# Reordering the branch units, output projection and first MLP pair of a one-core decoder layer

## The chip, the cores and the metric

The kernel runs on one core of a Trainium2 chip. The metric is the device time of one execution in microseconds (us), lower is better. Five engines work side by side, each through its own instruction stream: PE (TensorE, matrix products), DVE (VectorE), ACT (ScalarE), POOL (GpSimd) and SP (SyncE, which here only starts transfers). An engine runs its stream in order; an instruction that waits for another engine holds up everything behind it on its own.

## The reference

One decoder layer on x of 1024 positions by 1024 channels, float32. Two token mixers, gated and merged, are projected by w_out and added to x; a gated MLP with a causal convolution of width 3 follows.

```python
merged = (jax.nn.sigmoid(g_a) * (y_att @ w_oa[l])
          + jax.nn.sigmoid(g_b) * (y_sgu @ w_ob[l]))
x = x + merged @ w_out[l]
x = x + conv_gated_mlp(rmsnorm(x, ffn_norm[l]), w_up[l], conv_w[l], conv_b[l], w_down[l])
```

## The kernel before

Every large product is done in a form with 7 block products instead of 8 (Strassen's scheme in Winograd's form). The left operand, a weight, comes as the blocks A11, A12, A22 and the sums S1 to S4, the right operand as B11, B21, B22 and the sums T1 to T4. The results of the block products are added up on DVE and ACT into the four quarters of the output. Each factor is stored as a high part in a short format and the low rest of it, and a product is three matmuls (high by high, high by low, low by high), each 128x128 by 128x512. To **split** a tile means: ACT copies it into the short format (the high part, `copy_hi`, line 88), then DVE or POOL subtracts that from the tile (the low part). All weights' low parts are made on POOL.

The change touches three stages, which follow each other on PE.

**Branch units, u0 to u7** (`branch`, order in `B_UNITS`). Each computes two tiles of 128 output channels of one branch ("a" or "b") and multiplies them by the gate. A unit is two jobs, `first` (products A11, S3, A12, S1) and `second` (A22, S2, S4). The names follow the products: `x1` and `x7` are ACT's copies of the first two out of PSUM, `u2` that of a partial sum. A12 adds onto the bank that x1 copies, so PE can't begin A12 before the x1 copy (L1360) is done. In branch "a" (u2, u4, u6, u7) the unit's result must be added to branch "b"'s, tile by tile: `m_add` puts the sum into `mraw`, the merged activations. It does so late, in the first job of the next unit or, for u7, in output job 0 (`un["late"]`). `mraw` is the right operand of the output projection, so its blocks B11, B21, B22 and the sums T1 to T4 are formed from it (`m_sum`) and split (`m_split`), in halves 0 and 1 of two tiles each. Where such work stands in the streams is written by hand: `un["hooks"][u, 0]` and `[u, "x"]` run at two places of unit u's first job, `[u, 1]` at the end of its second, and `O_WORK[j]` in output job j.

**Output jobs 0 to 13** (`out_job`). Step s (0 to 6, `O_STEPS`) is one of the seven block products, job 2s + e does its tiles 2e and 2e + 1, with 24 matmuls. The results gather in two PSUM accumulators, pX and pY. `o_post` takes one to its end: `final` adds it (times plus or minus one half) to the tiles of x in `ac`, `keep` copies the new x back into `ac` and stores it to memory, and the gained tiles become the right operand of the MLP (`comb`): `right_hi`/`right_lo` for B21 and B22, `right_split` for B11, T1, T3, T2 and T4, held until then in the buffers A and B (tiles hA and hB) and in pX and pY. `square` squares the new x on ACT and adds it up on POOL, for the normalization. Job j also splits the weights of job j + 2 (`wjh` on ACT, `wjl` on POOL). In between stands the preparation of the first MLP pair's weights (`w0`): loads that add two blocks in memory, issued by POOL (`adds`), their sums `lr` (`sums_r`) and the splits ph/pl, s3h/s3l and qh/ql.

**The first MLP pair** (`first_pair`, then a pair of the steady kind that takes over from it). Products in order: A11·B11, S3·T3, S1·T1, A12·B21, S4·B22, S2·T2, A22·T4. ACT copies the first out (`x1f`), the second (`x7`) and the third (`u2`; both are `xu`), DVE subtracts x7 - u2 and adds x1f to the fourth (L1775), and S4·B22 adds onto that. `fax` is the low part of the weights for S2 and S4.

Jobs run in a fixed pattern (`run_jobs`): PE's matmuls of job i, the load of job i + 4, the split of job i + 2, and then what DVE and ACT do with the result.

## Time and profile before

| | |
|---|---|
| median of 3 runs | 1204.44 us (1203.92 to 1204.49) |
| profiled execution | 1206.05 us, its span 1204.0 us |
| mean granted clock of PE | 0.989 |
| PE, DVE, POOL, ACT busy | 97%, 72%, 55%, 49% of the span |

In span time the branch units take about 379 to 457 us, the output jobs 457 to 545, the first pair and the one behind it 545 to 611. From there on all MLP pairs run alike, up to the down projection at the end. In the rows that follow later, a line such as `pz<-y,wjh` says that the tile pz was written from y and wjh; x2 behind a shape is a group of two such instructions; a bracket says how long the engine had been idle and which engine and line ended that. "PE pz L1106 <- ACT x L1360: 5.1, 2, 2.6" is a wait: PE's product at line 1106 waited for ACT's copy at line 1360, 5.1 us in two times, the longest 2.6.

### The profile page before, as it was taken

Reading aid. Unit: us, or ns where it says so; the run is one execution under the profiler, and the core shown is the slowest. Engines: PE = TensorE matmul, PEld = TensorE weight load, DVE = VectorE, ACT = ScalarE, POOL = GpSimd, SP = SyncE. Lnnn points to the kernel's source line nnn. Section 1 sums busy time; section 2 is a strip of 40 time slices with the busy share of each in tenths; the row PEclk is TensorE's granted clock in tenths of the full one; section 3 lists DMA queues with packets and bytes.
Section 4 is the critical chain, followed back from the end, with each engine's and each line's share of the span. In section 5 each row is a group of like instructions: output and inputs, shape, how many; then the busy total and the mean of one; then the engine's idle time right before and its main releaser. Section 6 shows DMA issues by size and latency. Waiting matters only on the chain.

```text
span 1204.0 us, 15874 instructions
## 1 busy us (share of the span) xinstructions
PE 1169.4 (97%) x5784; PEld 985.9 (82%) x5784; DVE 860.9 (72%) x1007; ACT 592.5 (49%) x938; POOL 657.0 (55%) x460
## 2 busy tenths in 40 slices
PE   9999999999999999896999999999999999999998
PEld 9899999888888777684878888888888887888886
DVE  7777737635447779676487878878887798776674
ACT  6665668644346444656444444444444445435331
POOL 1677774688865545574877776767767541000000
PEclk9999999999999999998999999999999999999999
DMA  9332584175647645533454455545545257975561
GB/s 369 127 115 73 136 250 172 62 245 163 169 137 263 197 173 210 182 107 122 92 172 126 137 165 136 167 115 151 154 136 149 85 201 271 370 250 192 159 234 53
DMA packets 86430, 204.37 MB, mean 170 GB/s; under 512 B 9617, under 2 KB 17297, under 8 KB 86161
## 3 DMA queue, kind: packets, MB, share of 16 engines
q1 hardware_dynamic: 77280, 174.93, 42.0%
q0 software_dynamic: 8544, 19.93, 10.0%
q10 hardware_dynamic: 528, 8.52, 2.1%
q8 instruction: 45, 0.74, 0.2%
q14 instruction: 33, 0.26, 0.1%
HBM read 162.70 MB, written 57.41 MB: 183 GB/s over the span
## 4 chain that ended last, share of the span: by engine, by line
PE 71%; DVE 14%; ACT 5%; POOL 4%; issue 3%; DMA 2%; SPq 0%; DVEq 0%; ACTq 0%; POOLq 0%
PE pz L1106 42%; PE pd L1984 7%; PE pdx L1984 7%; PE pu L94 1%; PE pu L92 1%; PE pu L93 1%; PE pY L1632 1%; DVE tv L1682 1%; DVE tg L1682 1%; PE pq L92 1%; PE pq L94 1%; PE pq L93 1%; PE pv L560 1%; DVE pz L664 1%; DVE mraw L1440 1%
## 5 line engine op out<-in xcount | busy, mean ns | idle before, releaser
L1106 PE MATMUL pz<-T,qh 128*128 128x512 f32 x472 | 145.5, 390 | 0.0
L1106 PE MATMUL pz<-B,ph 128*128 128x512 f32 x352 | 110.9, 397 | 1.5 <-ACT x L1818 0.8
L1106 PEld LDWEIGHTS pz<-T,qh 128*128 128x128 f32 x472 | 88.4, 188 | 18.6 <-ACT u L930 0.3
L1065 POOL TENSOR_TENSOR pl<-lp,ph 128x1024 fp32r<-128x1024 f32 x30 | 73.3, 2443 | 49.7 <-ACT ph L88 49.7
L1106 PE MATMUL pz<-T,ql 128*128 128x512 f32 x236 | 91.8, 389 | 0.0
L1106 PEld LDWEIGHTS pz<-B,ph 128*128 128x128 f32 x352 | 65.6, 189 | 18.1 <-ACT x L1818 3.9
L1106 PE MATMUL pz<-T,s3h 128*128 128x512 f32 x232 | 72.9, 396 | 6.1 <-ACT x1f L1754 6.1
L1106 PE MATMUL pz<-y,wjh 128*128 128x512 f32 x224 | 72.0, 403 | 5.5 <-ACT x L1360 5.1
L1124 DVE TENSOR_TENSOR pz<-pz,rstd_b 128x1024 f32<-128x1024 f32 x60 | 73.9, 1232 | 4.6 <-ACT rstd_b L143 2.6
L1065 POOL TENSOR_TENSOR ql<-lq,qh 128x1024 fp32r<-128x1024 f32 x30 | 76.7, 2556 | 0.0
L1106 PE MATMUL pz<-B,pl 128*128 128x512 f32 x176 | 69.3, 394 | 2.3 <-POOL pl L1065 2.3
L1984 PE MATMUL pdx<-bh,al 128*128 128x512 f32 x176 | 68.7, 390 | 0.2 <-DVE al L1955 0.2
L1984 PE MATMUL pdx<-bh,ah 128*128 128x512 f32 x176 | 68.6, 390 | 0.1
L1984 PE MATMUL pdx<-bl,ah 128*128 128x512 f32 x176 | 68.5, 389 | 0.0
L1346 POOL TENSOR_TENSOR wjl<-wj,wjh 128x512 fp32r<-128x512 f32 (+1 forms) x32 | 40.3, 1279 | 45.1 <-ACT wjh L88 45.1
L1106 PE MATMUL pz<-T,AX 128*128 128x512 f32 x252 | 60.5, 389 | 0.0
L1106 PE MATMUL pz<-B,AX 128*128 128x512 f32 x252 | 60.5, 389 | 0.0
L1065 POOL TENSOR_TENSOR s3l<-lq,s3h 128x512 fp32r<-128x512 f32 x20 | 25.9, 1297 | 62.5 <-ACT s3h L88 62.5
L88 ACT ACTIVATE ah<-ra 128x1024 fp32r<-128x1024 f32 (+1 forms) x24 | 23.7, 988 | 68.8 <-DMA ra<-wdown 30.6
L1106 PEld LDWEIGHTS pz<-T,s3h 128*128 128x128 f32 x232 | 44.4, 192 | 16.1 <-ACT x1f L1754 6.8
L88 ACT ACTIVATE AX<-lr 128x1024 fp32r<-128x1024 f32 x21 | 22.3, 1063 | 71.1 <-POOL lr L664 71.1
L1682 DVE SCALAR_TENSOR_TENSOR tv<-pz,cp,tv 128x1023 f32<-128x1023 f32 (+1 forms) x44 | 56.2, 1278 | 0.8
(380 smaller groups left out, 3629.7 us busy)
## 6 DMA issues: line engine op xcount, KB each, us to landing
lp<-wup SPq DMA_DIRECT2D x22, 512.0 KB, 3.8
lq<-wup SPq DMA_DIRECT2D x22, 512.0 KB, 4.1
ra<-wdown SPq DMA_DIRECT2D x44, 256.0 KB, 4.4
b<-T SPq DMA_DIRECT2D x44, 256.0 KB, 3.4
lq<-wup POOLq DMA_DIRECT2D x42, 256.0 KB, 5.4
B<-tv SPq DMA_DIRECT2D x33, 256.0 KB, 2.0
T<-tt SPq DMA_DIRECT2D x33, 256.0 KB, 2.1
b<-B SPq DMA_DIRECT2D x33, 256.0 KB, 3.0
```

The source lines that it names most:

```text
L88: return nc.scalar.activation(dst, src, AF.Copy, scale=scale)
L92: nc.tensor.matmul(out, wh, mh, start=first, stop=False, **kw)
L93: nc.tensor.matmul(out, wh, ml, start=False, stop=False, **kw)
L94: nc.tensor.matmul(out, wl, mh, start=False, stop=last, **kw)
L560: nc.tensor.matmul(o, vhl[:, kb, g, :], w[:, 2 * g:2 * g + 2, :], start=i == 0 and g == 0, stop=i == len(ops) - 1, skip_group_check=True)
L664: eng.tensor_tensor(out, x, y, op=op)
L1065: nc.gpsimd.tensor_tensor(l, r, h.bitcast(F), op=ALU.subtract)
L1106: nc.tensor.matmul(o, p[:, k, :], m, start=not more and k == 0 and j == 0, stop=k == nk - 1 and j == 2, skip_group_check=True)
L1124: nc.vector.tensor_tensor(z, z, rstd_b, op=ALU.mult)
L1346: nc.gpsimd.tensor_tensor(l[:, k], r[:, k], h[:, k].bitcast(F), op=ALU.subtract)
L1682: nc.vector.scalar_tensor_tensor(t[:, j:], p[:, 0:1024 - j], cw[:, ci, 2 - j:3 - j], t[:, j:], op0=ALU.mult, op1=ALU.add)
L1984: nc.tensor.matmul(o[d], p[:, k - k0, m], q[:, k - k0, :], start=new and k == 0 and j == 0, stop=k == HK - 1 and j == 2, skip_group_check= ...
```

## The change

It moves operations to other places of the streams of ACT, DVE and POOL; the matmuls and their order stay.

- Branch units: the split of B11 and the T1 sum leave `m_add` for the end of the second job of the unit (`hooks[3, 1]`, `[5, 1]`), behind that unit's own sums; T1 is split at the end of u6 (`hooks[6, 1]`) instead of within u6's first job. B21 and the T2 sums go from `m_add` and u7's hook to output job 0.
- Output jobs: the sums for T3 and T4 go from job 2 to jobs 6 and 7, their splits to jobs 7 to 9; T2 is split in job 1; `w0.adds` goes from job 6 to 7, `split_s3` from 8 to 9, `sums_r` from 7 to 8.
- `final`, `keep`, `right_split`, `square` and the copies of pX to pY work on a pair of tiles (1024 columns) where they worked on one (512). The buffer `sqt` of the squares exists once, for a pair, where there were two for a tile each. The high part of an output weight is one copy instead of two.
- First pair: the four operations `B - g·22`, needed for T2, leave `o_post` for the place behind x1f and fax; `X + …`, needed for T4, goes behind the third product; T2's split goes behind x7's copy; a square stands behind fax, one behind u2's copy and one behind the fourth product.

```diff
@@ run_jobs
             if i == 16:
                 un["late"]()
+                m_lo("B21", 0)
+                for k in (slice(2, 3), slice(3, 4)):
+                    m_hi("B21", 1, k)
+                    m_lo("B21", 1, k)
+                m_sum("T2", 0)
+                m_sum("T2", 1)
@@ gates
-        un["hooks"][6, "x"] = lambda: m_split("T1", 0)
-        un["hooks"][6, 0] = lambda: m_split("T1", 1)
-        un["hooks"][7, 0] = lambda: (m_split("B22", 0), m_split("B21", 0))
+        un["hooks"][3, 1] = lambda: (m_split("B11", 0), m_sum("T1", 0))
+        un["hooks"][5, 1] = lambda: (m_split("B11", 1), m_sum("T1", 1))
+        un["hooks"][6, 1] = lambda: (m_split("T1", 0), m_split("T1", 1))
@@ m_add
-        if i == 0:
-            m_split("B11", g)
-        else:
-            if u == 7:
-                for e in (0, 1):
-                    m_split("B21", g, ks=slice(2 * g + e, 2 * g + e + 1))
-        m_sum(("T1", "T2")[i], g)
@@ square
-        if n in ("11", "12") and d == 0:
-            nc.scalar.activation(q, ob[n][:, d, :], AF.Square)
+        t = pools["fp"].tile([128, 2, 512], F, tag="sqt", name=nm("sqt"))
+        nc.scalar.activation(t, ob[n][:, 2 * e:2 * e + 2, :], AF.Square)
+        if n in ("11", "12") and e == 0:
+            nc.gpsimd.tensor_tensor(q, t[:, 0, :], t[:, 1, :], op=ALU.add)
         else:
-            t = pools["fp"].tile([128, 512], F, tag="sqt", name=nm("sqt"), bufs=2)
-            nc.scalar.activation(t, ob[n][:, d, :], AF.Square)
-            nc.gpsimd.tensor_tensor(q, q, t, op=ALU.add)
+            for k in (0, 1):
+                nc.gpsimd.tensor_tensor(q, q, t[:, k, :], op=ALU.add)
@@ O_WORK
-        0: lambda: (m_split("T2", 0), out_load("11"), out_load("21")),
-        1: lambda: (m_split("T2", 1), m_split("B22", 1), out_load("22")),
-        2: lambda: (m_sum("T3", 0), m_sum("T3", 1), m_sum("T4", 0), m_sum("T4", 1), out_load("12")),
-        3: lambda: m_split("T4", 0),
-        4: lambda: (square("11", 0), square("11", 1), w0.load_p(), w0.load_s3(), w0.load_q()),
-        5: lambda: (b11(0), b11(1), square("11", 2), square("11", 3)),
-        6: lambda: (b11(2), b11(3), w0.adds(), m_split("T4", 1)),
-        7: lambda: (m_split("T3", 0), w0.sums_r()),
-        8: lambda: (m_split("T3", 1), w0.split_s3()),
-        10: lambda: (square("12", 0), square("12", 1)),
-        11: lambda: (square("12", 2), square("12", 3)),
-        12: lambda: (square("22", 0), square("22", 1)),
-        13: lambda: (square("22", 2), square("22", 3)),
+        0: lambda: (m_hi("B21", 0), m_hi("B22", 0), out_load("11"), out_load("21")),
+        1: lambda: (m_split("T2", 0), m_split("T2", 1), m_lo("B22", 0), out_load("22")),
+        2: lambda: (m_split("B22", 1), out_load("12")),
+        4: lambda: (square("11", 0), w0.load_p(), w0.load_s3(), w0.load_q()),
+        5: lambda: (b11(0), square("11", 1)),
+        6: lambda: (b11(1), m_sum("T3", 0), m_sum("T3", 1)),
+        7: lambda: (m_split("T3", 0), w0.adds(), m_sum("T4", 0), m_sum("T4", 1)),
+        8: lambda: (m_split("T3", 1), m_split("T4", 0), w0.sums_r()),
+        9: lambda: (square("12", 0), m_split("T4", 1), w0.split_s3()),
+        10: lambda: square("12", 1),
+        12: lambda: square("22", 0),
@@ o_post, one tile at a time before, a pair after; steps 5 and 6
-            if s == 5:
-                right_lo("B22", d, Yb[d], gs[d][0])
-                stt(B[:, d, :], Yb[d], gs[d][1], B[:, d, :], ALU.subtract)
-                stt(Yb[d], Yb[d], gs[d][1], A[:, d, :], ALU.add)
-            if s == 6:
-                right_lo("B21", d, X[d], gs[d][0])
-                stt(X[d], X[d], gs[d][0], B[:, d, :], ALU.add)
+        if s in (5, 6):
+            m, p = ("B22", Yb) if s == 5 else ("B21", X)
+            for i, d in enumerate(ds):
+                right_hi(m, d, p[:, i, :], gs[i][0])
+            keep(n, e, p)
+            for i, d in enumerate(ds):
+                right_lo(m, d, p[:, i, :], gs[i][0])
+        if s == 5:
+            for i, d in enumerate(ds):
+                stt(Yb[:, i, :], Yb[:, i, :], gs[i][1], A[:, d, :], ALU.add)
@@ first_pair
         q.prod(q.v1, "A11", "B11")
-        for f in o_late:
-            f()
         nc.scalar.copy(x1, q.v1)
...
+        square("22", 1)
+        for d in range(4):
+            stt(ob["B"][:, d, :], ob["22"][:, d, :], gain("22", d)[1], ob["B"][:, d, :], ALU.subtract)
         nx.load_p()
         q.prod(q.v0, "S3", "T3")
-        for d in range(4):
-            right_split("T2", d, ob["B"][:, d, :], nc.vector)
         nc.scalar.copy(x7, q.v0)
+        for e in (0, 1):
+            right_split("T2", e, ob["B"][:, 2 * e:2 * e + 2, :])
...
         nc.scalar.copy(u2, q.g1)
+        square("21", 0)
+        for e in (0, 1):
+            for i in (0, 1):
+                d = 2 * e + i
+                p = ob["X"][e][:, i, :]
+                stt(p, p, gain("21", d)[0], ob["B"][:, d, :], ALU.add)
+            right_split("T4", e, ob["X"][e])
         sub(nc.vector, x7, x7, u2)
-        for d in range(4):
-            right_split("T4", d, ob["X"][d], nc.vector)
         q.prod(q.g0, "A12", "B21")
-        for d in range(4):
-            square("21", d)
+        square("21", 1)
```

The first place is DVE's stream around the second job of u3, whose merged rows come from u2. `mraw<-m,pz` are m_add's sums, `mB<-mraw,mB` is the low part of B11, `mraw<-mraw` the T1 sum, and from `pz<-x,pz` on these are the unit's own sums. Before:

```order
L1440 TENSOR_TENSOR mraw_4366<-m_4141,pz_4237 128x1024
L1440 TENSOR_TENSOR mraw_4366<-m_4143,pz_4238 128x1024
L1418 TENSOR_TENSOR mB_4369<-mraw_4366,mB_4369 128x1024
L664 TENSOR_TENSOR mraw_4366<-mraw_4366 128x2x512
L1380 TENSOR_TENSOR pz_4324<-x_562_4325,pz_4324 128x512
L664 TENSOR_TENSOR pz_4324<-pz_4324,u_564_4327 128x512
```

The same place of the changed kernel (its lines are numbered 6 to 13 higher):

```order
L1452 TENSOR_TENSOR mraw_4366<-m_4141,pz_4237 128x1024
L1452 TENSOR_TENSOR mraw_4366<-m_4143,pz_4238 128x1024
L1386 TENSOR_TENSOR pz_4324<-x_562_4325,pz_4324 128x512
L664 TENSOR_TENSOR pz_4324<-pz_4324,u_564_4327 128x512
L664 TENSOR_TENSOR pz_4324<-x_563_4326,pz_4324 128x512
L1392 TENSOR_TENSOR pz_4323<-u_564_4327,pz_4323 128x512
L1399 SCALAR_TENSOR_TENSOR m_4406<-th_4284,pz_4323 128x1024
L1399 SCALAR_TENSOR_TENSOR m_4408<-th_4286,pz_4324 128x1024
L1422 TENSOR_TENSOR mB_4410<-mraw_4366,mB_4410 128x1024
L664 TENSOR_TENSOR mraw_4366<-mraw_4366 128x2x512
```

The low part of B11 and the T1 sum moved behind all six of the unit's operations; on ACT the high part moved with them, from ahead of u2's copy to right ahead of the next x1 copy.

The second place is DVE's stream in output jobs 6 to 9. `ac<-pY,ac` is job 6's and 7's final, `mT` the low parts of T3 and T4. Before:

```order
L1418 TENSOR_TENSOR mT_5007<-mraw_4707,mT_5007 128x1024
L1513 SCALAR_TENSOR_TENSOR ac_4848<-pY_4895,ac_4848 128x512 x2
L1418 TENSOR_TENSOR mT_667_5185<-mraw_4366,mT_667_5185 128x1024
L1513 SCALAR_TENSOR_TENSOR ac_4848<-pY_4896,ac_4848 128x512 x2
L1418 TENSOR_TENSOR mT_667_5185<-mraw_4366,mT_667_5185 128x1024
L1513 SCALAR_TENSOR_TENSOR pY_4895<-pY_4895,ac_4848 128x512 x2
```

Changed:

```order
L664 TENSOR_TENSOR mraw_4366<-mraw_4706,mraw_4366 128x2x512 x2
L1525 SCALAR_TENSOR_TENSOR ac_4839<-pY_4888,ac_4839 128x1024
L1422 TENSOR_TENSOR mT_666_5149<-mraw_4366,mT_666_5149 128x1024
L668 SCALAR_TENSOR_TENSOR mraw_4706<-mraw_4366,mraw_4706 128x2x512 x2
L1525 SCALAR_TENSOR_TENSOR ac_4839<-pY_4889,ac_4839 128x1024
L1422 TENSOR_TENSOR mT_666_5149<-mraw_4366,mT_666_5149 128x1024
L1422 TENSOR_TENSOR mT_5190<-mraw_4706,mT_5190 128x1024
L1525 SCALAR_TENSOR_TENSOR pY_4888<-pY_4888,ac_4839 128x1024
```

The T4 split (`mT_5007`) that stood ahead of job 6's final is gone from there (`mT_5190` now stands behind job 7's); in its place stand the T3 sums (L664), and between the two finals the T4 sums (L668).

The third place is DVE's stream in the first pair, from the last final on. `T_704` (`T_700` after) is T2, `T_707` (`T_704` after) is T4. Before:

```order
L1513 SCALAR_TENSOR_TENSOR pX_4850<-pX_4850,ac_4847 128x512 x2
L1499 SCALAR_TENSOR_TENSOR B_694_5444<-pX_4850,cp,B_694_5444 128x512
L1526 SCALAR_TENSOR_TENSOR pX_4850<-pX_4850,cp,hB 128x512
L1499 SCALAR_TENSOR_TENSOR B_694_5444<-pX_4850,cp,B_694_5444 128x512
L1526 SCALAR_TENSOR_TENSOR pX_4850<-pX_4850,cp,hB 128x512
L1492 TENSOR_TENSOR T_704_5541<-hB,T_704_5541 128x512 x4
L664 TENSOR_TENSOR xu<-xu 128x512
L1492 TENSOR_TENSOR T_707_5572<-pX_4849,T_707_5572 128x512 x2
L1492 TENSOR_TENSOR T_707_5572<-pX_4850,T_707_5572 128x512 x2
L1775 TENSOR_TENSOR pz_5506<-pz_5506,x1f 128x512
```

Changed:

```order
L1525 SCALAR_TENSOR_TENSOR pX_4841<-pX_4841,ac_4838 128x1024
L1510 SCALAR_TENSOR_TENSOR B_691_5385<-pX_4841,cp,B_691_5385 128x512 x2
L1539 SCALAR_TENSOR_TENSOR hB<-ac_4839,sink_b,hB 128x512 x4
L1503 TENSOR_TENSOR T_700_5478<-hB,T_700_5478 128x1024 x2
L1539 SCALAR_TENSOR_TENSOR pX_4840<-pX_4840,cp,hB 128x512 x2
L1503 TENSOR_TENSOR T_704_5509<-pX_4840,T_704_5509 128x1024
L1539 SCALAR_TENSOR_TENSOR pX_4841<-pX_4841,cp,hB 128x512 x2
L1503 TENSOR_TENSOR T_704_5509<-pX_4841,T_704_5509 128x1024
L664 TENSOR_TENSOR xu<-xu 128x512
L1773 TENSOR_TENSOR pz_5434<-pz_5434,x1f 128x512
```

All four `hB` operations and all of `X + …` now follow the last final, and the sum `xu` stands behind T4's low parts instead of ahead of them.

More of the change, by code (lines that the diff above doesn't have):

```diff
@@ L1415, in m_split @@
         k = ks or slice(2 * g, 2 * g + 2)
[L1416 to L1418 removed]
+        copy_hi(mb[n][:, 0, k], m_part(n)[:, k])
     def m_sum(n, g):
@@ L1473, in open_out @@
         ob["11"], ob["21"], ob["12"], ob["22"] = y[:, 0], y[:, 1], z[:, 0], z[:, 1]
-        ob["X"] = [p[:, c] for p in (PS("pX"), PS("pX")) for c in (L, H)]
+        ob["X"] = [PS("pX").rearrange("p (d c) -> p d c", d=2) for _ in range(2)]
     HK = NPAIR // 2
@@ L1643, in main @@
             if s == 0:
-                for d in ds:
-                    nc.scalar.copy(ob["Y"][d], ob["X"][d])
+                nc.scalar.copy(ob["Y"][e], ob["X"][e])
             else:
-                o_post(s, ds)
+                o_post(s, e)
             if j == 13:
```

106 lines of the change are left out of this document (47 added, 59 removed).

## The prediction

> **What bounds the kernel now.** I read the page's busy times first, then the waits of TensorE (PE), then its windows, because a loss that can be won back must show as time in which PE stands still or runs slowly.
>
> ```profile
> PE 1169.4 (97%) x5784; PEld 985.9 (82%) x5784; DVE 860.9 (72%) x1007; ACT 592.5 (49%) x938; POOL 657.0 (55%) x460
> ```
>
> PE is busy for 97% of the span, so nothing is won by making another engine's work cheaper, except where PE waits for it. The change lies between about 400 and 610 us. This is the waits view for 390 to 660 us: the PE line that waits, the line that released it, us in total, times, longest.
>
> ```profile
> PE pz L1106 <- ACT x1f L1754: 6.1, 1, 6.1
> PE pz L1106 <- ACT x L1360: 5.1, 2, 2.6
> PE pY L1632 <- DVE ac L1513: 3.0, 1, 3.0
> PE pz L1106 <- POOL pl L1065: 2.3, 1, 2.3
> PE pz L1106 <- DVE pz L1775: 2.2, 1, 2.2
> PE pY L1632 <- ACT pY L1645: 2.2, 1, 2.2
> PE pX L1632 <- POOL wjl L1547: 1.1, 1, 1.1
> PE pX L1632 <- ACT wjh L88: 0.7, 1, 0.7
> PE pz L1106 <- ACT xu L1766: 0.7, 1, 0.7
> ```
>
> These are 23.4 us. A wait also has an aftermath. The next rows are 3.5 us windows that begin where PE resumes after a wait; columns are length, PE busy (matmuls), granted clock, DMA share, GB/s.
>
> ```profile
> 415.65:419.20 3.55, 3.55 (x9) 0.53 0.32 87
> 470.81:474.40 3.59, 3.58 (x16) 1.00 0.61 226
> 510.80:514.40 3.60, 3.58 (x9) 0.55 0.23 93
> 548.10:551.70 3.60, 3.56 (x10) 0.58 0.18 67
> 558.36:561.90 3.54, 3.54 (x8) 0.50 0.92 255
> 571.89:575.40 3.51, 3.51 (x10) 0.60 0.01 5
> ```
>
> At full clock 3.59 us hold 16 matmuls, 0.224 us each. After five of the waits they hold 8 to 10: 6 to 8 matmuls too few, 1.3 to 1.8 us, take 1.6. The wait at 470.81 (2.2 us) left no such mark. So the second L1360 wait and the wjh/wjl pair, whose windows I don't quote, are also charged 1.6 each.
>
> The Trainium skill, "TensorE: Matmul & The Clock Gate", Part 1, says that the array falls to 4/8 after about one idle window of 3.4 us, and that this window runs freely. The 0.50 of 558.36 agrees with 4/8. Waits of 2.2 to 3.0 us with the mark, and one of 2.2 without, agree with a free-running window only if less than a full window of idling is enough. Strictly by the page only the waits over 3.4 us, x1f and the g0 + x1 expected below, would be followed by a slow stretch; the other aftermaths, 4 x 1.6 + 2 x 1.3 = 9.0, would not be there to be won, and the sum would be 15.8 - 9.0 = 6.8. The windows of before measure them, so this gets no chance.
>
> **Loss of before, in order.** L1360 at u4 and u6: 5.1 + 2 x 1.6 = 8.3. pY: 2.2. wjh and wjl: 1.8 + 1.6 = 3.4. ac: 3.0 + 1.6 = 4.6. pl: 2.3 + 1.3 = 3.6. x1f: 6.1 + 1.8 = 7.9. xu: 0.7. pz L1775: 2.2 + 1.3 = 3.5. Together 34.2 us.
>
> **Branch units.** The chain behind the first L1360 wait, from the timelines of DVE and ACT (start, us, engine, line):
>
> ```profile
> 406.98 2.34 DVE L1440 TENSOR_TENSOR mraw<-m,pz 128x1024 f32<-128x1024 f32 x2
> 409.36 1.06 ACT L88 ACTIVATE mB<-mraw 128x1024 fp32r<-128x1024 f32 x1 [2.08 <-DVE mraw L1440]
> 410.52 1.23 DVE L1418 TENSOR_TENSOR mB<-mraw,mB 128x1024 fp32r<-128x1024 f32 x1 [1.20 <-ACT mB L88]
> 411.78 1.22 DVE L664 TENSOR_TENSOR mraw<-mraw 128x1024 f32<-128x1024 f32 x1
> 412.93 0.69 DVE L1380 TENSOR_TENSOR pz<-x,pz 128x512 f32<-128x512 f32 x1
> 413.70 0.58 ACT L1381 COPY u<-pz 128x512 f32<-128x512 f32 x1 [3.28 <-DVE pz L1380]
> 414.18 0.94 ACT L88 ACTIVATE wjh<-wj 128x512 fp32r<-128x512 f32 x2
> 415.02 0.57 ACT L1360 COPY x<-pz 128x512 f32<-128x512 f32 x1
> ```
>
> DVE ends the merged rows at 409.32, waits 1.2 for ACT's high half of B11, then does the low half and the T1 sum. Only then comes the unit's own sum at 412.93, behind which u2, the weight split and the x1 copy follow on ACT. The change puts that split and sum behind the unit's sums. L1380 can start at 409.32, 3.6 us earlier. The high half of B11 (1.06) now stands right ahead of the x1 copy on ACT and gives back 1.06. Net 2.55, against waits of 2.6 and 2.5: both go, and with nothing over 0.1 left their aftermaths go too, **8.3 saved**. If 0.5 of each were left, 1.0 less. The low half and the T1 sum (1.2 each) then run on DVE while PE does the next unit's first products.
>
> What is late next is u7: its x1 copy stands behind both T1 high halves, 2 x 1.06, on ACT, which start only behind u6's last sums. At u4 a delay of 3.6 made a wait of 2.6, so such a copy has 1.0 of slack: a wait of 2.1 - 1.0 = **1.1**. Bounds: 0, and 2.1 + 1.6. POOL's splits and PE's matmuls keep their order in the units.
>
> **Output jobs, 0 to 8.** The T3 and T4 sums leave jobs 2 for 6 and 7, and of what filled jobs 0 to 2 only T2's split, B21's halves and B22's stay there, so that B21, T2 and the PSUM copies are ready when jobs 2 to 4 want them. That removes pY (2.2). wjh and wjl (3.4) were late because m_lo, m_sum and the splits filled ACT and DVE ahead of them; about 0.4 stays, since a pY copy is now behind T2's high halves. Bounds 0 and 1.5. **5.2 saved.** The 3.0 wait on ac has its cause in one row:
>
> ```profile
> 478.53 4.54 DVE L668 SCALAR_TENSOR_TENSOR mraw<-mraw,mraw 128x1024 f32<-128x1024 f32 x2
> 504.54 4.94 DVE L1418 TENSOR_TENSOR mT<-mraw,mT 128x1024 fp32r<-128x1024 f32 x1
> 504.01 0.92 POOL L1023 DMA_DIRECT2D s<-wup  x1
> 504.62 1.22 POOL L1024 DMA_DIRECT2D lq<-wup  x1
> 505.20 3.19 POOL L1547 TENSOR_TENSOR wjl<-ow,wjh 128x512 fp32r<-128x512 f32 x2
> ```
>
> The low half of T4 took 4.94 instead of 1.23 (the same line at 410.52): it was issued while POOL issued two loads, and ended after two POOL splits. With w0.adds moved to job 7 and T4's split to jobs 8 and 9, the two no longer meet there, and job 8's final stands ahead: 4.6 go. Whether another DVE operation meets the loads at job 7 (two T4 sums stand next to them) is the largest unknown: 0 or 3.7 (4.94 - 1.23). I take 0 as the likelier, because in the row at 478.53 two such sums beside POOL cost 2.27 each, 1.05 above the plain 1.22, not 3.7. **4.6 saved.**
>
> **Output jobs 9 to 13.** PE is now some 17 us early, and the chain final, copy, split, final on DVE and ACT sets the pace. What was waited for at job 8 is now spread. Merging two tiles into one instruction gives little:
>
> ```profile
> L1418 DVE TENSOR_TENSOR mB<-mraw,mB 128x1024 fp32r<-128x1024 f32 x5 | 6.0, 1220 | 2.3 <-ACT mB L88 2.3
> L1492 DVE TENSOR_TENSOR T<-pY,T 128x512 fp32r<-128x512 f32 x4 | 2.7, 686 | 1.3 <-ACT T L88 1.3
> L1526 DVE SCALAR_TENSOR_TENSOR hB<-pY,sink_b,hB 128x512 f32<-128x512 f32 x8 | 5.8, 743 | 2.4 <-ACT ac L1509 2.3
> ```
>
> One 1024 costs 1.22, two 512 cost 1.37; 0.15 a pair. Some 25 pairs give under 4 us on DVE, none of it on PE's path by itself. A pair also makes its first half wait for its second, 0.6 us. I put the two against each other at nothing. The tile stores on SP stay as many and go two at a time; the loads behind them on SP's queue keep their order, and the weight loads are issued two jobs ahead of their split, which covers a store that comes 0.6 later. The low half of job 11's weights now stands on POOL behind the add of square 12 and s3's low half (2 x 1.3 by the adds' 5.34 / 4 in the next block of rows; I let a lead of 1.0 hide its part), and job 12's weights follow it: two new waits, **1.6 and 0.7**, without aftermath. Bounds 0 and 2.3 + 1.6. The four B - g22 operations and four of X that leave steps 5 and 6 (8 x 0.74 = 5.9) let DVE reach the last final earlier; ph's low half is in place and pl no longer waits: **3.6 saved**.
>
> **First pair.** These are the rows that end its three waits:
>
> ```profile
> 554.14 1.42 DVE L1513 SCALAR_TENSOR_TENSOR pX<-pX,ac 128x512 f32<-128x512 f32 x2
> 557.69 0.62 ACT L1754 COPY x1f<-pz 128x512 f32<-128x512 f32 x1
> 560.63 3.44 DVE L1492 TENSOR_TENSOR T<-hB,T 128x512 fp32r<-128x512 f32 x4
> 559.34 2.38 POOL L1065 TENSOR_TENSOR fax<-lr,fax 128x1024 fp32r<-128x1024 f32 x1 [2.42 <-ACT fax L88]
> 571.10 5.34 POOL L1523 TENSOR_TENSOR sq<-sq,sqt 128x512 f32<-128x512 f32 x4 [9.38 <-ACT sqt L1522]
> 571.15 0.69 DVE L1775 TENSOR_TENSOR pz<-pz,x1f 128x512 f32<-128x512 f32 x1
> ```
>
> x1f stands on ACT behind the last B21 halves and the kept tile. From the last final (554.14) to the end of x1f (558.31) is 4.2 us. In the changed kernel that final can start about 2 us after the last matmul of job 13, ends PE's wait 6 us after it, and 12 matmuls (2.7) of the first product cover a part: **3.5 + 1.8** stay of 7.9.
>
> Behind it stands what was moved here. DVE: four B - g22 (3.0), T2's low halves (2.4), X (3.0), T4's (2.4), the sum x7 (0.7) and g0 + x1 (0.7). Before, B - g22 and X were done step by step behind the finals, ahead of x1f. The chain from T2's low half: X 1.4, ACT high 1.06, low 1.2, X 1.4, high 1.06, low 1.2, two sums 1.4: 8.7 us, against two products (24 matmuls, 5.4) that PE has meanwhile. With the start of that chain about 1 to 3 late behind fax and the squares' adds, xu waits **0.7 to 3.1** and g0 + x1 **4 to 7**, together about 7.7 plus one aftermath, **1.6**. Before it was 0.7 + 3.5.
>
> By the Trainium skill, "SBUF — State Buffer", the section on two separate sides, a DVE operation with two SBUF inputs and a GpSimd operation that reads SBUF take the shared port exclusively, and whoever starts first keeps it. That speaks against this move: B - g22, the T4 sums and T2's low halves get neighbours on POOL. The 2.27 of the sums and 0.86 each of the T2 halves (3.44 / 4, against 0.69) agree in kind.
>
> **Sum.** Saved 8.3 + 5.2 + 4.6 + 3.6 - 1.1 - 2.3 = 18.3 up to the first pair. First pair: 7.9 - 5.3 = 2.6 saved, and 4.2 - 9.3 = -5.1. Net 18.3 + 2.6 - 5.1 = 15.8 us. Behind the first pair the waits are those of before. The profiled execution took 1206.05, its span 1204.0, so 2.05 lie around it, and it is 1.6 above the median of 1204.44. The span becomes about 1188 and the median 1204.4 - 15.8 = **1188.6**.
>
> **Rivals.**
>
> *A. The jobs tie up DVE again.* A T4 sum at job 7 starves as at 504.54 (3.7), or u7's x1 copy is late by the full bound (2.6 more). For it: the same kind of operation stands beside the same loads. Against: one instance in the trace. Price 2.6 to 5.3 us, the upper with an aftermath: 1191 to 1194, middle 1193.
>
> *B. The chain from job 9 on is latency bound, and only what lies in the branch units survives.* PE's lead is then eaten by the first pair: 8.3 saved, 1196. For it: all of B - g22 and X (5.9 us) now follows the last final on DVE. Against: that final comes earlier by it.
>
> *C. Better.* The pairs on DVE and ACT hide the new waits in jobs 9, 10 and u7 (3.4), and g0 + x1 waits only 4 (about 2): up to 5.4 more. 1183 to 1186.
>
> *D. Slower.* In the first pair ACT's square has one buffer, so it waits for two POOL adds (2.6) each time, three times, with T4's high halves behind it, and the port turns add up to fax and six adds (2.38 + 8 = 10.4) on DVE. Together 18.2, against 15.8 saved: 1206.8. It decides from the point where g0 + x1 ends later than now, 571.84, against the 552 to 556 that I expect. Against it: the first square can start long before T4 is due, so most adds run in PE's lead.
>
> *E. No change (within 0.2%, 2.4 us, about what a measurement of this kernel can tell):* D at a part of its price.
>
> **Chances.** Forecast 0.50 (own range 1186 to 1191), A 0.20, B 0.12, C 0.10, D 0.04, E 0.04. Faster 0.92, same 0.04, slower 0.04. From 1182 (a little below C) to 1198 (B with its bounds) about 0.85 is held; the bounds of the unknown costs reach no further.
>
> **What would show it.** No PE wait on the x1 copies of u4 and u6; one of under 1 us at u7. No DVE operation of 4.9 us beside the POOL loads. PE resumes job 8's work near 493.5 instead of 510.8. x1f ends near 535 to 537 instead of 558.3, and g0 + x1 is the longest wait of the first pair, 4 to 7. It would be wrong if a T4 sum takes over 4 us, if u7's wait is over 2, or if g0 + x1 waits over 9.

## The result, and the profile after

The changed kernel takes 1192.04 us (median of 4 runs, 1191.43 to 1194.49) against 1204.24 of the kernel before (4 runs). The ratio is 0.9903, with a 95% interval of 0.9885 to 0.9920: 12.2 us faster, where 15.8 were forecast. The profiled execution took 1194.49, its span 1192.6; it is the slowest of the four.

The waits of PE in the profile after, 390 to 650 us (PE's line, the line that released it, us in total, times, longest; L1112 is L1106 of before):

```profile
PE pz L1112 <- DVE pz L1773: 5.2, 1, 5.2
PE pz L1112 <- ACT xu L1760: 3.3, 1, 3.3
PE pz L1112 <- ACT x1f L1745: 3.0, 1, 3.0
PE pX L1628 <- POOL wjl L1560: 2.3, 2, 1.9
PE pY L1628 <- DVE ac L1525: 1.4, 1, 1.4
PE pz L1112 <- ACT x L1366: 0.6, 1, 0.6
PE pY L1628 <- ACT pY L1638: 0.2, 1, 0.2
```

The two x1 waits (5.1) are gone, and 0.6 stands at u7. Of the output jobs' waits (pY, wjh, wjl, ac, pl, 9.3) 4.1 are left (wjl 2.3, ac 1.4, pY 0.2, and pl 0.2, whose row isn't shown). The three in the first pair were x1f 6.1, xu 0.7 and pz 2.2, together 9.0, and are now 3.0, 3.3 and 5.2, together 11.5.

Where the time was won and given back is read best by setting the same matmul of both traces side by side. I count matmuls from the start of the span and subtract their start times. The second profile of the changed kernel (run e1_again, span 1189.7) is used, because the first one had lost 0.95 us already before 392 us, ahead of all that was changed. The columns are the start times in us and the lead over the profile before:

```
place (matmul number)            before    after     lead
A12 of u4 (2488)                 415.65    412.89     2.8
output job 0 (2644)              457.42    449.48     7.9
output job 8 (2836, 2860)        510.82    493.56    17.3
                                 517.99    500.55    17.4
first pair, third matmul (2980)  545.19    531.73    13.5
behind x1f (2992)                558.36    537.15    21.2
third product (3004)             563.06    541.31    21.8
A12.B21 (3016)                   566.65    547.50    19.2
S4.B22 (3028)                    571.89    558.22    13.7
normalization (3052)             579.08    565.74    13.3
last of the span (5783)         1198.87   1184.51    14.4
```

The lead grows to 17.4 by job 8, loses 4 in jobs 9 to 13, is won back at pl and x1f, and falls from 21.8 to 13.7 within two products of the first pair, 13.3 at the normalization. At the end it is more than 12.2 mostly because the profiled execution of before was 1.8 above its median and that of e1_again 1.0 below its own. These are the windows there, of the first profile after (length, PE busy with matmuls, granted clock, DMA share, GB/s), each from where PE resumes:

```profile
538.12:541.62 3.50, 3.50 (x10) 0.59 0.93 281
548.47:553.30 4.83, 4.83 (x11) 0.50 0.00 0
559.20:564.40 5.20, 5.20 (x12) 0.50 0.56 77
```

Behind the u2 wait and behind the g0 + x1 wait a whole product each runs at half clock. What they wait for stands in the timelines of DVE, POOL and ACT of the same profile (start, us, engine, line, written <- read):

```profile
538.94 6.92 DVE L1539 SCALAR_TENSOR_TENSOR hB<-ac,sink_b,hB 128x512 f32<-128x512 f32 x4
539.10 2.82 POOL L1071 TENSOR_TENSOR fax<-lr,fax 128x1024 fp32r<-128x1024 f32 x1 [2.89 <-ACT fax L88]
541.88 3.43 POOL L1536 TENSOR_TENSOR sq<-sq,sqt 128x512 f32<-128x512 f32 x2
545.95 2.00 ACT L88 ACTIVATE T<-hB 128x1024 fp32r<-128x1024 f32 x2 [2.87 <-DMA lq<-wup]
547.86 0.57 ACT L1760 COPY xu<-pz 128x512 f32<-128x512 f32 x1
558.46 0.69 DVE L1773 TENSOR_TENSOR pz<-pz,x1f 128x512 f32<-128x512 f32 x1
```

The four B - g22 take 6.92 us beside POOL's fax and square, and not evenly (shortest, median and longest in ns):

```profile
L1539 DVE SCALAR_TENSOR_TENSOR hB<-ac,sink_b,hB x4: 743/1774/2870, 538.9 to 544.1; 128x512 f32<-128x512 f32 x4
```

The first starts 0.16 us ahead of fax and takes 0.74. The other three take 2.87, 1.78 and 1.77: each ends 0.55 behind the end of the POOL operation that was running. The four end at 545.86, and T2's high halves start at 545.95; the bracket names a load, which came in at about the same time, but the operand is hB. The u2 copy is right behind them on ACT. X, T4 and g0 + x1 follow on DVE up to 559.15.

And in the output jobs, DVE and POOL:

```profile
493.57 6.65 DVE L668 SCALAR_TENSOR_TENSOR mraw<-mraw,mraw 128x1024 f32<-128x1024 f32 x2
494.74 0.92 POOL L1029 DMA_DIRECT2D s<-wup  x1
495.35 1.22 POOL L1030 DMA_DIRECT2D lq<-wup  x1
495.92 3.20 POOL L1560 TENSOR_TENSOR wjl<-ow,wjh 128x512 fp32r<-128x512 f32 x2
```

The two T4 sums take 6.65. The second alone takes 4.42 of it; it starts at 495.80, while POOL issues its loads, and POOL's next two splits follow. It ends 1.10 behind the end of the second split, just as the T4 low half did in the profile before.

### The profile page after: what moved, and what is told of

Its sections match the earlier page's. It is cut to its first block, busy times and chain, and to the rows that moved or that the text cites. A ratio compares the mean times of both kernels' runs of the same rounds, so it can differ in the third digit from the quotient of the medians.

```text
span 1192.6 us, 15813 instructions
## 1 busy us (share of the span) xinstructions
PE 1165.1 (98%) x5784; PEld 983.2 (82%) x5784; DVE 859.7 (72%) x985; ACT 588.6 (49%) x894; POOL 665.5 (56%) x460
## 4 chain that ended last, share of the span: by engine, by line
PE 77%; DVE 9%; POOL 6%; ACT 3%; issue 3%; DMA 2%; SPq 0%; POOLq 0%; DVEq 0%; ACTq 0%
PE pz L1112 43%; PE pdx L1982 9%; PE pd L1982 8%; DMA lq<-wup 2%; PE pY L1628 1%; PE pX L1628 1%; PE pu L94 1%; PE pu L92 1%; PE pu L93 1%; PE pvs L93 1%; PE pvs L92 1%; PE pvs L94 1%; POOL lr L664 1%; PE pq L92 1%; PE pq L94 1%
## 5 line engine op out<-in xcount | busy, mean ns | idle before, releaser
L1112 PE MATMUL pz<-T,qh 128*128 128x512 f32 x472 | 145.5, 390 | 0.0
L1112 PE MATMUL pz<-B,ph 128*128 128x512 f32 x352 | 111.6, 399 | 3.9 <-ACT xu L1760 3.3
L1112 PEld LDWEIGHTS pz<-T,qh 128*128 128x128 f32 x472 | 88.5, 188 | 18.6 <-ACT u L936 0.3
L1112 PE MATMUL pz<-T,ql 128*128 128x512 f32 x236 | 91.8, 389 | 0.0
L1112 PEld LDWEIGHTS pz<-B,ph 128*128 128x128 f32 x352 | 66.1, 191 | 20.6 <-ACT xu L1760 3.7
L1112 PE MATMUL pz<-T,s3h 128*128 128x512 f32 x232 | 72.5, 394 | 3.0 <-ACT x1f L1745 3.0
L1112 PE MATMUL pz<-y,wjh 128*128 128x512 f32 x224 | 69.7, 391 | 0.9 <-ACT x L1366 0.6
L1112 PE MATMUL pz<-B,pl 128*128 128x512 f32 x176 | 69.7, 396 | 0.2 <-POOL pl L1071 0.2
L1112 PE MATMUL pz<-T,AX 128*128 128x512 f32 x252 | 60.5, 389 | 0.0
L1112 PE MATMUL pz<-B,AX 128*128 128x512 f32 x252 | 60.5, 389 | 0.0
L88 ACT ACTIVATE ah<-ra 128x1024 fp32r<-128x1024 f32 (+1 forms) x24 | 23.7, 988 | 68.9 <-DMA ra<-wdown 31.2
L1675 DVE SCALAR_TENSOR_TENSOR tg<-pz,cp,tg 128x1023 f32<-128x1023 f32 (+1 forms) x44 | 56.2, 1278 | 0.8
```

What stands on the lines that cost most here:

```text
L88: return nc.scalar.activation(dst, src, AF.Copy, scale=scale)
L1112: nc.tensor.matmul(o, p[:, k, :], m, start=not more and k == 0 and j == 0, stop=k == nk - 1 and j == 2, skip_group_check=True)
L1675: nc.vector.scalar_tensor_tensor(t[:, j:], p[:, 0:1024 - j], cw[:, ci, 2 - j:3 - j], t[:, j:], op0=ALU.mult, op1=ALU.add)
```

## The experiments

Theory: the branch units and the output jobs give what was forecast; the first pair gives back more than forecast, because operations that read two tiles in SBUF on DVE were put beside POOL's work, and because X, T4 and T2 were queued ahead of the two operations that PE needs. Rivals: later chains on DVE and ACT eat any lead; the pairing gives the gain; forming T2 and T4 in the first pair is what lets the lead through. All times stand beside the kernel before, measured with them on the same chip (7 runs each): 1205.38 for e1_again to e4_g0_first, 1204.69 for e5_hole to e8_hole_g0_first, 1205.37 for e9_fp_undone to e11_all. Each variant has 4 runs. Variants of different groups are compared by what each saves against the kernel before.

**e1_again: the changed kernel once more.**

> The changed kernel itself, once more, so that the others have a profile beside them on the same chip. Both theories expect 1191 to 1193 us and the same waits as in the first profile: g0 + x1 5.2, u2 3.3, x1f 3.0, ac 1.4, with two slow stretches of 12 to 13 matmuls behind the u2 and the g0 + x1 wait. The extra 0.95 us that the first profile had lost already before the changed region should not be there again if it is chance.

1192.58 us (1191.54 to 1193.28), 12.8 less. The waits are the same within 0.3, but for g0 + x1, 6.3 here, and x1f, 2.5. The 0.95 us ahead of the region is not there. The operations again: T4 sums 6.66, B - g22 6.92. The stretch behind the u2 wait is shorter, with a granted clock of 0.68 in its first 3.5 us instead of 0.50.

**e2_branch: the branch units alone.**

```diff
-        un["hooks"][6, "x"] = lambda: m_split("T1", 0)
-        un["hooks"][6, 0] = lambda: m_split("T1", 1)
+        un["hooks"][3, 1] = lambda: (m_split("B11", 0), m_sum("T1", 0))
+        un["hooks"][5, 1] = lambda: (m_split("B11", 1), m_sum("T1", 1))
+        un["hooks"][6, 1] = lambda: (m_split("T1", 0), m_split("T1", 1))
```

(and m_add without these two; everything else as before)

> The kernel before with the moves in the branch units alone (B11 split and T1 sum to the ends of u3 and u5, T1 split to the end of u6). Theory 1, each stage keeps what it gains: the two x1 waits and their slow stretches go, a wait of about 0.6 stays at u7, 8 us saved, about 1196.3. Theory 2, the later stages are bound by chains on DVE and ACT that eat a lead: 1200 or more, and larger waits at pY, ac and x1f than before.

1196.84 us (1193.97 to 1198.81), 8.5 less. Waits of this kernel:

```profile
PE pz L1106 <- ACT x1f L1753: 6.1, 1, 6.1
PE pY L1631 <- DVE ac L1512: 3.1, 1, 3.1
PE pY L1631 <- ACT pY L1644: 2.2, 1, 2.2
PE pz L1106 <- ACT x L1361: 0.6, 1, 0.6
```

x1f, pY and ac are those of before to 0.1 (wjh and wjl, 1.8, are gone, and a wait of 0.8 stands elsewhere), so the lead passes whole through the jobs and the first pair. Theory 1 is right. Rival B of the prediction isn't tested by this run, since it too keeps the gain of the branch units.

**e3_bg22_back: B - g22 back in step 5.**

```diff
                 right_lo(m, d, p[:, i, :], gs[i][0])
+                if s == 5:
+                    stt(B[:, d, :], Yb[:, i, :], gs[i][1], B[:, d, :], ALU.subtract)
```

(and the four taken out of the first pair)

> The changed kernel with the four operations B - g22 back behind the finals of step 5. Theory 1, they cost 6.9 us instead of 3.0 in the first pair because they share the port with fax and the square's adds on POOL: out of there they take 0.75 each, the u2 wait falls from 3.3 to under 1, g0 + x1 from 5.2 to about 3, x1f comes up to 3 later; in sum 2 to 4 us less, 1188 to 1190. Theory 2, the tail is set by the chain of copies and splits and not by the port: the u2 wait stays at 2 or more and the time gets longer by what x1f loses, 1193 to 1195.

1192.36 us (1191.91 to 1193.37): no change, so neither number was right. The parts came as theory 1 has them: each B - g22 takes 0.74, and the u2 wait is 0.7. But x1f's wait is 4.3, so the second product ends later, and T2's high halves stand on ACT behind x7's copy of it:

```profile
544.87 0.58 ACT L1753 COPY xu<-pz 128x512 f32<-128x512 f32 x1 [3.66 <-PE pz L1112]
545.36 2.01 ACT L88 ACTIVATE T<-hB 128x1024 fp32r<-128x1024 f32 x2
546.45 2.36 DVE L1503 TENSOR_TENSOR T<-hB,T 128x1024 fp32r<-128x1024 f32 x2 [6.18 <-ACT T L88]
```

T2's low halves start at 546.45, against 546.06 in e1_again, and with them X, T4 and g0 + x1, for which PE now waits 7.3. What the place beside POOL's work cost is won, and x1f takes it.

**e5_hole: B - g22 in DVE's idle place ahead of B21's last low halves.**

```diff
             keep(n, e, p)
+            if s == 6 and e:
+                for d in range(4):
+                    stt(B[:, d, :], ob["22"][:, d, :], gain("22", d)[1], B[:, d, :], ALU.subtract)
             for i, d in enumerate(ds):
                 right_lo(m, d, p[:, i, :], gs[i][0])
```

(and the four taken out of the first pair)

> The changed kernel with the four operations B - g22 between the last tile that is kept and B21's last low halves on DVE, where DVE was idle for 2.2 us and POOL nearly so. Theory 1, in the changed kernel they cost 6.9 us because of fax and the square on POOL, and that holds T2's high halves, behind them the u2 copy: here about 0.75 each, T2's high halves right behind x7's copy (near 543), the u2 wait falls from 3.0 to about 0.7 and loses its slow stretch, x1f does not move; 2.5 to 4 us less than the changed kernel, 1188.5 to 1190. Theory 2, what is won at u2 comes back in full at g0 + x1, since X and T4 stand ahead of it as before: the time stays within 1 us of 1192.5.

1189.28 us (1189.21 to 1190.23), 15.4 less than before and, by these differences, 2.6 less than the changed kernel.

```profile
534.53 3.46 DVE L1539 SCALAR_TENSOR_TENSOR hB<-ac,sink_b,hB 128x512 f32<-128x512 f32 x4
538.35 2.38 POOL L1071 TENSOR_TENSOR fax<-lr,fax 128x1024 fp32r<-128x1024 f32 x1 [2.90 <-ACT fax L88]
542.49 2.01 ACT L88 ACTIVATE T<-hB 128x1024 fp32r<-128x1024 f32 x2
555.00 0.69 DVE L1774 TENSOR_TENSOR pz<-pz,x1f 128x512 f32<-128x512 f32 x1
L1539 DVE SCALAR_TENSOR_TENSOR hB<-ac,sink_b,hB x4: 741/742/1467, 534.5 to 537.2; 128x512 f32<-128x512 f32 x4
```

The same four operations take 3.46 instead of 6.92 (the first 1.47, up to 0.55 behind the end of POOL's ql, the others 0.74 with POOL idle), and g0 + x1 comes 2.5 earlier than the 557.48 of e1_again. x1f is not touched (3.0). This is the price of the place beside fax and the square. PE still waits 7.4 for g0 + x1, since it is at the door earlier.

**e4_g0_first: the two operations that PE needs ahead of the others.**

```diff
         nc.scalar.copy(x7, q.v0)
-        for e in (0, 1):
-            right_split("T2", e, ob["B"][:, 2 * e:2 * e + 2, :])
...
         nc.scalar.copy(u2, q.g1)
+        for e in (0, 1):
+            right_split("T2", e, ob["B"][:, 2 * e:2 * e + 2, :])
         square("21", 0)
+        q.prod(q.g0, "A12", "B21")
+        nc.vector.tensor_tensor(q.g0, q.g0, x1, op=ALU.add)
         for e in (0, 1):
...
```

> The changed kernel with the u2 copy ahead of T2's split and g0 + x1 ahead of X and T4, all work kept. Theory 1, the u2 and g0 + x1 waits are a matter of what stands ahead of them on ACT and DVE: the u2 wait goes, g0 + x1 waits 1 to 2, at most one slow stretch is left, and the normalization or T4 waits 1 to 3 behind them: about 6 us less than the changed kernel, 1185 to 1187. Theory 2, the first pair is bound by the whole amount of DVE's work or by its loads: the wait comes back at T4 in full and the time stays within 2 us of 1192.

1188.22 us (1186.62 to 1188.75), 17.2 less than before and 4.4 less than the changed kernel beside it (about 6 were expected). Waits: u2 0.7, g0 + x1 2.5, and a new one of 2.9, the normalization waiting for the last square's adds, which stand behind T4 on ACT. B - g22 still take 6.93 in this run. By the medians, order alone, with that cost left in place, is worth more than the 2.6 of the place beside POOL's work; the intervals of the two ratios, 0.9839 to 0.9869 here and 0.9854 to 0.9887 in e5_hole, overlap, so which is larger isn't certain.

**e8_hole_g0_first: both, with both squares of 21 ahead of T4.**

```diff
 (both diffs above, and)
         square("21", 0)
         q.prod(q.g0, "A12", "B21")
+        square("21", 1)
         nc.vector.tensor_tensor(q.g0, q.g0, x1, op=ALU.add)
         for e in (0, 1):
             for i in (0, 1):
...
-            right_split("T4", e, ob["X"][e])
+        for e in (0, 1):
+            right_split("T4", e, ob["X"][e])
```

> Both moves together, B - g22 in DVE's idle place and, as in the run before, u2 ahead of T2's split, g0 + x1 ahead of X and T4, and in addition both squares of 21 ahead of T4's high halves on ACT. Theory 1: u2 waits 0.7, g0 + x1 at most 1.5, the wait for the squares of 2.9 falls to under 1, T4 is waited for up to 2; 3 to 5 us less than 1188.2, 1183 to 1185. Theory 2, the order in the first pair is exhausted and the work on DVE behind the last final sets the end: within 1 us of 1188.

1183.97 us (1180.68 to 1185.07), 20.7 less than before. u2 waits 0.7, g0 + x1 0.9, and the wait for the squares is gone, as theory 1 has it. A new wait of 2.6 stands in the next pair, and one more operation is stretched:

```profile
555.84 4.28 DVE L664 TENSOR_TENSOR xu<-xu 128x512 f32<-128x512 f32 x1
555.32 0.89 POOL L1029 DMA_DIRECT2D s<-wup  x1
555.91 1.22 POOL L1030 DMA_DIRECT2D lq<-wup  x1
556.49 3.07 POOL L1071 TENSOR_TENSOR pl<-lp,ph 128x1024 fp32r<-128x1024 f32 x1
```

x7 - u2, 0.69 in a free place, takes 4.28, with the same neighbours as the two cases above.

**e10_x7_early: e8_hole_g0_first with x7 - u2 right behind g0 + x1.**

```diff
         nc.vector.tensor_tensor(q.g0, q.g0, x1, op=ALU.add)
+        sub(nc.vector, x7, x7, u2)
...
             right_split("T4", e, ob["X"][e])
-        sub(nc.vector, x7, x7, u2)
```

> The faster version of before (B - g22 in the idle place, u2 and g0 + x1 first, squares of 21 first) with the subtraction x7 - u2 right behind g0 + x1 instead of behind T4. Theory 1, it took 4.28 us there because it was issued while POOL issued two accumulating loads and a split followed: here 0.7 to 1.9, the normalization's first step on DVE 2 us or more earlier, 0 to 2 us less. Theory 2, it is slow wherever POOL works and the loads of the next pair set what follows: still over 3, or no change of time.

1183.30 us (1182.24 to 1184.87), 22.1 less. The subtraction took 1.17 and the first DVE step of the normalization came at 558.01 instead of 560.03, as theory 1 has it. Between this run and e8_hole_g0_first the times themselves overlap.

**e6_adds_job6: the accumulating loads one job earlier.**

```diff
-        6: lambda: (b11(1), m_sum("T3", 0), m_sum("T3", 1)),
-        7: lambda: (m_split("T3", 0), w0.adds(), m_sum("T4", 0), m_sum("T4", 1)),
+        6: lambda: (b11(1), m_sum("T3", 0), m_sum("T3", 1), w0.adds()),
+        7: lambda: (m_split("T3", 0), m_sum("T4", 0), m_sum("T4", 1)),
```

> The changed kernel with POOL's two accumulating loads issued in job 6 instead of 7. Theory 1, the second T4 sum (both 6.66 us, against 3.4 to 4.5 for such pairs beside POOL) starves because it is issued while POOL issues these loads: two T4 sums of 2.3 or less each, no ac wait at job 8 (1.4), or another operation of DVE with two inputs in SBUF is hit in its place and is 2 us or more too long; 0 to 1.5 us less. Theory 2, the sums are long from the splits on POOL alone: both sums together stay above 6, whatever the loads do.

1190.87 us (1188.54 to 1192.00), 13.8 less than before, 1.0 less than the changed kernel.

```profile
492.14 4.55 DVE L668 SCALAR_TENSOR_TENSOR mraw<-mraw,mraw 128x1024 f32<-128x1024 f32 x2
487.69 0.91 POOL L1029 DMA_DIRECT2D s<-wup  x1
488.30 1.20 POOL L1030 DMA_DIRECT2D lq<-wup  x1
```

The T4 sums take 4.55 instead of 6.65 and the ac wait of 1.4 is gone. The T3 sums beside the moved loads took 3.45 for two, the same as in the changed kernel: no other operation was hit, though the second of them was issued while POOL issued a load. The runs of this kernel scatter by 3.5, so that 1.0 is not much to go by; the two profiles, 1188.54 and 1191.54, are 3.0 apart.

**e7_final_halves: each final in two halves.**

```diff
-        nc.vector.scalar_tensor_tensor(out, p, 0.5 * sign, ob[n][:, 2 * e:2 * e + 2, :], op0=ALU.mult, op1=ALU.add)
+        for i in (0, 1):
+            nc.vector.scalar_tensor_tensor(out[:, i, :], p[:, i, :], 0.5 * sign, ob[n][:, 2 * e + i, :], op0=ALU.mult,
+                                           op1=ALU.add)
```

> The changed kernel with each final done on two tiles one after the other instead of on a pair (12 DVE instructions more). Theory 1, pairing is worth about 0.2 us an operation and lies beside the order: time within 1 us of the changed kernel, up to 1 more where finals are on the path (jobs 8 to 13). Theory 2, the pairs are where the gain comes from: 3 us more or worse.

1190.58 us (1189.70 to 1193.47), 14.1 less than before, so not slower than with pairs; the intervals of the two ratios overlap. Halves cost up to 0.2 more (1.42 for two on PSUM against 1.22), but here POOL's loads began 1.2 ahead of the T4 sums instead of 1.2 behind their start, and the sums took 3.45. For the finals, the rival that the pairs give the gain is out. The pairs of keep, right_split, square and the copies were not undone in any run.

**e9_fp_undone: the first pair's part undone.** B - g22 and X + ... go back behind the finals of steps 5 and 6, T2's split ahead of x7's copy, x7 - u2 ahead of T4, both squares of 21 behind the fourth product. (The second square of 22 stays in the first pair.)

```diff
                 right_lo(m, d, p[:, i, :], gs[i][0])
+                if s == 5:
+                    stt(B[:, d, :], Yb[:, i, :], gs[i][1], B[:, d, :], ALU.subtract)
+                else:
+                    stt(p[:, i, :], p[:, i, :], gs[i][0], B[:, d, :], ALU.add)
...
         q.prod(q.v0, "S3", "T3")
-        nc.scalar.copy(x7, q.v0)
+        square("22", 1)
         for e in (0, 1):
             right_split("T2", e, ob["B"][:, 2 * e:2 * e + 2, :])
+        nc.scalar.copy(x7, q.v0)
...
         nc.scalar.copy(u2, q.g1)
-        square("21", 0)
+        sub(nc.vector, x7, x7, u2)
         for e in (0, 1):
...
             right_split("T4", e, ob["X"][e])
-        sub(nc.vector, x7, x7, u2)
         q.prod(q.g0, "A12", "B21")
+        square("21", 0)
         square("21", 1)
```

> The changed kernel with the first pair's part undone: B - g22 and X + ... back behind the finals of steps 5 and 6, T2's split ahead of x7's copy, x7 - u2 ahead of T4, the two squares of 21 behind the fourth product; operations on pairs stay. Theory 1, the branch units and the jobs give the gain, and the moves in the first pair give nothing or cost a little (x1f earlier by 3, u2 and g0 + x1 later by 5 with two longer slow stretches): 1191 to 1193, with x1f waited for 5 or more, g0 + x1 2 to 4. Theory 2, forming T2 and T4 in the first pair is what lets the lead through: 1195 or more.

1186.92 us (1186.08 to 1187.58), 18.5 less than before and 5.7 less than the changed kernel by these differences. Both expectations were wrong: the part was expected to be neutral or a gain, and it is a loss. Its waits:

```profile
PE pz L1112 <- ACT x1f L1749: 5.8, 1, 5.8
PE pz L1112 <- POOL pl L1071: 1.5, 1, 1.5
PE pz L1112 <- DVE pz L1771: 0.9, 1, 0.9
PE pz L1112 <- ACT xu L1762: 0.7, 1, 0.7
```

x1f and pl wait 4.1 longer than in the first profile after, u2 and g0 + x1 6.9 less, and of the three slow stretches only the one behind x1f is left (0.57). So the change splits into -8.5 for the branch units (e2_branch), -10.0 for the jobs with the pairs and +5.7 for the first pair. The second is only the rest of -18.5, and the third the rest of -12.8: the jobs were not run alone.

**e11_all: e10_x7_early with the loads in job 6.**

> The run e10_x7_early and, in addition, the accumulating loads in job 6. Theory 1, the two add up: the ac wait (1.4) goes as in the run with the loads alone, 1.5 to 2.5 less than e10_x7_early, about 1180 to 1182. Theory 2, waits behind the first pair (loads for the next one, 2.6 at its x copy) take it back: within 0.7 of e10_x7_early.

1181.70 us (1180.68 to 1182.74), 23.7 less than before, ratio 0.9803 (0.9788 to 0.9817): the best of all, 1.6 below e10_x7_early as theory 1 has it. It splits T2 and forms T4 in the first pair like the changed kernel, so that idea is not what costs; the places are. The ac wait is gone; x1f (3.0) and wjl (1.9) are the largest that stay.

## Why the prediction was right, and where not

The direction was right, and 1192.0 lies in the range of 1182 to 1198, but the sum of 15.8 was 3.6 too large: the time lies outside the forecast's own 1186 to 1191 and inside rival A's 1191 to 1194. That it lies there is luck. A's mechanism did come, and with it one of the prediction's own signs of being wrong ("if a T4 sum takes over 4 us": 4.42), but it cost about 1.4 and not 2.6 to 5.3. The first pair lost 3.3 more than was charged.

- **Branch units, 8.3 less 1.1 at u7.** Right: 7.9 of lead at job 0, where 7.2 were forecast, and 8.5 alone. u7 waited 0.6. The chain was the one described: L1386 starts right behind m_add, and ACT's high half of B11 stands ahead of the x1 copy:

```profile
410.19 0.69 DVE L1386 TENSOR_TENSOR pz<-x,pz 128x512 f32<-128x512 f32 x1
412.29 1.05 ACT L88 ACTIVATE mB<-mraw 128x1024 fp32r<-128x1024 f32 x1
413.24 0.57 ACT L1366 COPY x<-pz 128x512 f32<-128x512 f32 x1
```

- **Jobs 0 to 8, 5.2 and 4.6.** Right in sum: 17.4 of lead against 17.0, with errors that cancel. The branch units gave 0.7 more, and from job 0 to the start of job 8 the lead grew by 9.3 where 8.2 were charged (5.2 and the ac wait's 3.0). And "two T4 sums stand next to them ... 0 or 3.7 ... I take 0 as the likelier" fell the other way: the second sum starved, and 1.4 of wait came back at job 8, without a slow stretch. That was rival A's mechanism; e6_adds_job6 took the starving and the wait away, worth 1.0 there and 1.6 in e11_all.
- **Jobs 9 to 13, -2.3.** The waits were 2.3 (1.9 and 0.4) in the first profile and 2.0 in e1_again, at the named place, POOL's wjl behind the square and s3's low half. In e1_again a slow stretch of 1.9 came on top, which the prediction had only in its bounds; in the first profile there was none. Which of the two comes is chance, as the last section shows. pl, 3.6, was won: 0.2 is left.
- **x1f, 3.5 + 1.8.** Slightly better: 3.0 and 2.5 in two profiles. The lead behind it, 21.2, is what the sum gave (14.7 + 3.6 + 2.6 = 20.9).
- **The tail of the first pair, -5.1: the term that was mis-sized.** It measured -8.4 (21.75 to 13.34): in e1_again 48 matmuls, 10.8 at 0.224 each, took 24.4 there, so 13.7 were lost where 9.3 were reckoned, and in the profile before 16.0, so 5.3 where 4.2 were reckoned. Of the waits, u2 and g0 + x1, 7.7 was charged, from 0.7 to 3.1 and from 4 to 7; 8.5 and 9.3 came in the two profiles, u2 (3.3 and 3.0) at its upper end. The prediction put the B - g22 at "four B - g22 (3.0)" and the lateness behind fax and the squares at "about 1 to 3". They took 6.9, and in e5_hole, mostly out of POOL's way, 3.5: 3.5 to 3.9 late. So g0 + x1 ended at 558.2 in e1_again against the 552 to 556 expected. The rest is the slow stretches. One of 1.6 was counted; two came, in the first profile of 11 to 12 matmuls at 0.50, which is 2.4 to 2.5 each (4.83 - 11 x 0.224, 5.20 - 12 x 0.224). The stretch behind u2 costs nothing by itself, since at S4 DVE was later than PE; the one behind g0 + x1 is up to 0.9 above what was counted. So the first pair did eat a part of the lead, as rival B had it, but 13.3 of 21.8 passed.
- **The rule of the Trainium skill, "SBUF — State Buffer", the section on two separate sides**, that spoke against the move, was weighed in a sentence and left out of the sum. Measured, the B - g22 agree with it: the first, issued ahead of fax, took 0.74, and fax behind it 2.82 instead of the 2.38 of e5_hole; the other three each ended 0.55 behind a POOL operation. X, which reads one of its two tiles from PSUM, took 1.55 for two at 549.32 in the first profile, with a square's adds on POOL from 549.46 on, and was not held.

## What to carry to other kernels

Behind a stage that has just been made faster, queue first what TensorE waits for next, and put what is needed two products later behind it: that order alone was worth 4.4 us here, with the contention left in place. When an operation moves, price it with its new neighbours: a VectorE operation with two SBUF operands that takes 0.74 us alone was held until GpSimd's running operation was done and took 1.8 to 2.9; taking four of them out of there was worth 2.6 us. And split a change into its parts before judging it: two parts gained 18.5 us and the third gave 5.7 back.

## What the runs showed of the hardware

The slow stretch after a wait is not a function of the wait's length alone. In the 13 profiles every slow stretch between 405 and 615 us consists of whole pieces of 3.41 us with a granted clock of 0.50. In each profile these pieces lie on one grid of 3.41 us, which falls differently from profile to profile. What counts is how long PE stands within one piece of that grid. The wait on job 11's wjl shows it. It was 1.95 to 1.96 us in eight profiles. In four of them (e1_again, e3_bg22_back, e4_g0_first, e8_hole_g0_first) it lay whole in one piece, and the next piece was slow, 9 matmuls instead of 15 or more. Here are both pieces of e1_again (length, PE busy with matmuls, granted clock, DMA share, GB/s):

```profile
511.21:514.62 3.41, 1.45 (x7) 1.00 0.36 139
514.62:518.03 3.41, 3.41 (x9) 0.50 0.47 88
```

In the other four the same wait lay across a border of the grid, and nothing followed, as in the first profile after:

```profile
510.24:513.65 3.41, 2.87 (x13) 1.00 0.74 279
513.65:517.06 3.41, 2.00 (x9) 1.00 0.00 0
517.06:520.48 3.42, 3.42 (x17) 1.00 0.86 244
```

Over all 13 profiles in that stretch of time, a piece at full clock in which PE stood for 1.87 us or more was followed by a slow one each time (39 pieces), and one with 1.57 or less never, but for one in e10_x7_early, where PE stood for 0.33 and spent 1.95 on the normalization's 16 products of two columns. So the border lies between 1.57 and 1.87 here. It explains two waits that left no mark, the 2.2 us in the profile before (1.56 and 0.62 in two pieces) and the 2.6 at x1f in e4_g0_first (1.27 and 1.30). A slow piece costs at most half of its length, 1.7 us. That a piece's border counts and not the wait's begin fits the freely running window of the Trainium skill, "TensorE: Matmul & The Clock Gate", Part 1, but less idling than the whole window that it asks for was enough. When a slow piece is followed by a second one isn't settled by these numbers. The grid may also be part of why runs of one kernel differ by 1 to 5 us; no run tested that.

A VectorE operation with two SBUF operands that was issued while POOL issued two accumulating loads, with a split queued right behind, took 4.3 to 4.9 us instead of 0.7 to 1.2 in three places: the T4 low half before (4.94), the second T4 sum after (4.42), x7 - u2 in e8_hole_g0_first (4.28). Each was issued before POOL's next operation began (0.66, 0.12 and 0.65 us) and yet ended 1.10, 1.10 and 0.56 behind the last POOL operation of the group, which is about its own free time: POOL went first with all that it had queued. Such loads don't always do it. In e6_adds_job6 the second T3 sum was issued at 488.74, during the second load (488.30 to 489.50) and 0.14 ahead of the split, and took 1.21; the split took 2.23. In e7_final_halves a T4 sum was issued at 494.17, also during the loads (493.01 to 494.85), and took 1.21. What decides who goes first stays open.
